# Experts summed by tokens, factors brought to the places by products, one more weight region, wider router products

## The chip, the cores and the metric

The kernel runs on one core of a Trainium2 chip. The metric is the device time of one execution in microseconds (us), as the median of several runs. The engines are TensorE (PE in the rows; its weight loads are PEld), VectorE (DVE), ScalarE (ACT), GpSimd (POOL) and SyncE (SP), which issues all transfers here.

## The reference, cut to what matters

Two transformer-like blocks are applied to a stream of 256 tokens with 1024 features: a gated mixer and a feed-forward part under conditioning, then pooling and sparse attention, cross attention to a memory, and a layer of experts. The change touches mostly the last:

```python
h = rmsnorm(x, ffn_norm)
g_sel = argmax(h @ wg_router + bg)                     # one of 4 groups
e_in  = (h @ we_router + be)[g_sel]                    # 8 experts of that group
top_w = softmax(top2(e_in)) * softmax(g_logits)[g_sel] # two experts a token, with weights
hid   = silu(h @ w_gate[e]) * (h @ w_up[e])            # 1024 -> 256, for each of 32 experts
x     = x + sum over the token's two experts of top_w * (hid @ w_down[e])
```

All is float32. The weights of all 32 experts are read, whichever tokens choose them.

## The kernel before

Weights are read once, in order, from one long array ("stream" in DRAM, the list PLAN) into regions: R0 to R25, 26 buffers of 128 x 2048 float32 (1 MB each, NREG at L247). The same regions hold activations: the stream of tokens by features (xt), its transposed copy (ht), the gathered places (xg) and so on. A region is free again when its last reader is done. Small work buffers are two tiles U (512 wide), tiles s, and T pieces of a region; B are the eight PSUM banks.

All instructions of the program are first recorded and then put in order by a planner (plan, L589, and flush, L763): for each engine it picks the next instruction by modelled times and priorities. PATH (L830) lists seeds that perturb the priorities from pass to pass; the last pass counts. Transfers keep their recorded order on SyncE. A transfer may be issued ahead as long as a region is left for all buffers that come before its use. Where the planner sees a wait on TensorE it puts in fillers, products of a matrix of ones that nobody reads (filler, L795; their rows have L800). As all is issued from one helper, nearly all other rows have L823.

The work around the change: the sum of squares is turned into a norm factor per token by norm_col (L1115), with products of one column. After the cross attention, rf is that factor; the router's products (40 columns: 4 groups, 4 empty, 32 experts) of xt are scaled by it. xt is transposed to ht (L1823), scaled by rf on the way out of PSUM. VectorE chooses the experts (asum marks them), products with a triangle of ones count the places, and places (L1886) makes a 0/1 table s8 of tokens by places: each of 32 experts has CAP = 32 places. There are eight groups of four experts. For each group, experts (L1940) does:

- gather (L1921): products of ht with s8 bring the tokens to their places (xg), features by places;
- the gate and up weights, eight regions, as tiled products (four experts side by side, 32 columns of the array each), silu and product to hid;
- two transposes, then the down weights, four regions, as tiled products to ye, places by features;
- combine (L1934): products of ye with the table of weights (w8 = s8 times the weight of the token, transposed) add into four PSUM banks, features by tokens.

After the last group the sum is added to xt in four parts and written. SyncE reads the number of rounds (more than one only if an expert has over 32 tokens, which does not happen here) at L2029.

Early in the program, the conditioning sums (ada_pe, ada_v) go through a U tile each; group means and head factors are products with constant matrices (blk, sel, dup, perm) from the constants cst.

Of the kernel before, what the change touches and what calls it, by code (L numbers as in the profile page):

```python
# [15 lines left out]
KT = D // 128  # L16
# [7 lines left out]
    ("c", 8), ("norm1_g", 8), ("b_u", 4), ("b_val", 4), ("b_gate", 4), ("taps", TAPS), ("taps4", 96),  # L24
# [7 lines left out]
for _n, _w in VEC:  # L32
# [5 lines left out]
    ("ident", 128), ("e4", 4), ("same", 32), ("blk", 128), ("perm", 128), ("dup", 128), ("triu", 128),  # L38
    ("iota", 32), ("half", 2), ("sel", 512), ("thr", 8),
# [9 lines left out]
def constants():  # L49
# [9 lines left out]
    put("blk", (p[:, None] // 64 == p[None, :] // 64) / 64.0)  # L59
    put("perm", (p[:, None] == (p[None, :] ^ 32)))  # L60
    put("dup", (p[:, None] == p[None, :] % 64))
# [3 lines left out]
    sel = (np.arange(8)[:, None, None] == 2 * np.arange(4)[None, :, None] + p[None, None, :] // 64)  # L65
    put("sel", sel.reshape(8, 512))
# [18 lines left out]
def rope_tables():  # L85
    f = np.float32
    inv = (f(10000.0) ** (-(np.arange(0, 64, 2, dtype=f)) / f(64))).astype(f)
# [4 lines left out]
    return np.concatenate([np.tile(cos, (2, 1)), np.tile(sin, (2, 1))], axis=1).astype(f)  # L92


def layout(v):
# [14 lines left out]
    def rowk(w):  # L110
# [12 lines left out]
        "taps": taps[0], "taps4": taps4,  # L123
# [23 lines left out]
    for name, arg in PLAN:  # L147
# [60 lines left out]
        "wr": wr.reshape(KT, 128, 40).transpose(1, 0, 2), "br": br,  # L208
# [38 lines left out]
NREG = 26  # L247
# [120 lines left out]
def cost(eng, name, args, kw):  # L368
# [7 lines left out]
    if eng == "tensor":  # L376
# [4 lines left out]
        if "tile_position" in kw:  # L381
            return mv.free() * passes / 2.4e3 + 0.01
# [447 lines left out]
PATH = (0, 0, 11, 0, 63, 67, 74, 0, 89, 239)  # L830
# [9 lines left out]
def _build(tc, a, out, ctx):  # L840
# [11 lines left out]
    rec = Recorder(nc, {"R": [region(i) for i in range(NREG)], "U": tiles(2, "U", 512),  # L852
# [71 lines left out]
    inv_d = fixed(1, "inv_d")  # L924
    G.memset(inv_d, 1.0 / D)
    inv_a = fixed(1, "inv_a")
    G.memset(inv_a, 1.0 / DA)
# [151 lines left out]
    class Sums:  # L1079


        def __init__(self):
            self.acc, self.n = [], 0

        def add(self, src):
            i = self.n % 2
            self.n += 1
            if self.n <= 2:
                self.acc.append(buf("T", T))
            acc = self.acc[i]  # L1090
            if self.n <= 2:
                S.activation(out=acc, in_=src, func=AF.Square)
                return
# [4 lines left out]
    def rstd(out_, in_):  # L1098
        S.activation(out=out_, in_=in_, func=AF.Sqrt, bias=eps[0:in_.shape[0], 0:1])
# [15 lines left out]
    def norm_col(accs, inv, r=None):  # L1115
# [7 lines left out]
        rstd(r, ps[:, 0:2])  # L1123
# [124 lines left out]
    def stacked(i):  # L1248


        o = VOFF["taps4"] + 32 * i
        w = view(rtaps[i // 2], 1024 * (i % 2), 32, 32)
        V.tensor_tensor(out=w, in0=cs("same").unsqueeze(1).to_broadcast([128, 32, 32]),
                        in1=cv[:, o:o + 32].unsqueeze(2).to_broadcast([128, 32, 32]), op=ALU.mult)
# [3 lines left out]
    def memory():  # L1258
# [6 lines left out]
        rmem = norm_col(sums.acc, inv_d, rmem_)  # L1265
# [35 lines left out]
    S.activation(out=rb, in_=norm_bc(norm_col(sums.acc, inv_d)), func=AF.Copy)  # L1301
    xr = view(Reg(), 0, KT, T)
    rtaps = [Reg(), Reg()]
    wtaps = [stacked(i) for i in range(3)]
# [43 lines left out]
    def conv_v():  # L1348
        for i in range(TAPS):
            w, src = col("taps", i), ypad[:, i:i + T]  # L1350
# [67 lines left out]
    def mix():  # L1418
# [15 lines left out]
        bc = norm_bc(norm_col(suma.acc, inv_a))  # L1434
# [7 lines left out]
    def gn():  # L1442
        sq4 = view(r1, 0, 4, T)
        for j in range(4):
            ps = bank()[:, 0:T]
            PE.matmul(out=ps, lhsT=cs("blk"), rhs=yc[:, j], start=True, stop=True)
# [10 lines left out]
        normed(y, 4, yc, 4, "on_b", norm_bc(norm_col(sumb.acc, inv_a)))  # L1457
# [26 lines left out]
    r2_ = norm_col(sq2.acc, inv_d)  # L1484
# [39 lines left out]
    rbf = norm_bc(norm_col(sqf.acc, inv_d))  # L1524
# [18 lines left out]
    cosin = view(ri_, 1152, 2, T)  # L1543
    SY.dma_start(out=cosin, in_=a["cosin"].rearrange("p (a n) -> p a n", a=2))
# [4 lines left out]
    rmx = norm_col(sqx.acc, inv_d)  # L1549
# [12 lines left out]
    def rope(dst, src, t=None):  # L1562

        if t is None:
            sw = bank()[:, 0:T]
            PE.matmul(out=sw, lhsT=cs("perm"), rhs=src, start=True, stop=True)
# [9 lines left out]
    def key_index():  # L1576
# [3 lines left out]
        PE.matmul(out=pd, lhsT=cs("dup"), rhs=zk, start=True, stop=True)  # L1580
# [169 lines left out]
    wr, br = view(rq_, 1024, KT, 40), view(rq_, 1024 + KT * 40, 40)  # L1750
    SY.dma_start(out=wr, in_=a["wr"])
    SY.dma_start(out=br, in_=a["br"])
    for k in range(KT):
        V.tensor_scalar(out=wr[:, k], in0=wr[:, k], scalar1=col("fn", k), scalar2=None,
                        op0=ALU.mult)
# [11 lines left out]
    rx_ = norm_col(sq4_.acc, inv_d)  # L1767
# [56 lines left out]
    rf = norm_col(sq5.acc, inv_d)  # L1824
    pl = bank()
    lgt = small3(40, "lgt")
    for t in range(2):
        for k in range(KT):
            PE.matmul(out=pl[:, 64 * t:64 * t + 40], lhsT=xt[:, k, 128 * t:128 * t + 128],
                      rhs=wr[:, k], start=(k == 0), stop=(k == KT - 1))  # L1830
    for t in range(2):
        V.scalar_tensor_tensor(out=lgt[:, t], in0=pl[:, 64 * t:64 * t + 40],
                               scalar=rf[:, t:t + 1], in1=br, op0=ALU.mult, op1=ALU.add)
    for t in range(2):
        for i in range(2):
# [217 lines left out]
```

## Time and profile before

| | us |
|---|---|
| median of 3 runs (736.33 to 739.46) | 736.53 |
| the profiled execution | 738.67 |
| its span, first to last instruction | 737.0 |
| TensorE busy in the span | 703.4 |
| VectorE, ScalarE busy | 415.0, 314.0 |
| moved by the transfers | 212.45 MB |

The span is what the views show; the 1.67 us beside it lie before and after. Busy times overlap, so they are no sum. A matmul's row begins where it is issued, and its end is modelled. The granted clock (PEclk) is the share of the 2.4 GHz that TensorE was given: 1.00 or 0.50.

### The profile page before, as it was taken

The page shows a single profiled execution, that of the slowest core. Times are in us where ns is not written, and L with a number is a line of the kernel's source. Part 1 is how long each engine was busy: PE and PEld are TensorE (multiplying, and loading weights), DVE is VectorE, ACT ScalarE, POOL GpSimd, SP SyncE. Part 2 cuts the span into 40 slices and gives each one's busy share as a digit, 9 for nine tenths or more (in the row PEclk, how much of TensorE's full clock was granted, in tenths as well). Part 3 has the DMA queues.
Part 4 walks back from the last instruction along what each step waited for, and adds up shares of the span by engine and source line. Part 5 has one row for each costly group of instructions (what it writes and reads, how often), then busy time and mean ns, then how long its engine had stood idle before and what let it go on. Part 6 is the DMA issues. An engine that isn't in the chain of part 4 may idle for free.

```text
span 737.0 us, 13178 instructions
## 1 busy us (share of the span) xinstructions
PE 703.4 (95%) x5374; PEld 560.9 (76%) x5374; DVE 415.0 (56%) x873; ACT 314.0 (43%) x595; POOL 3.0 (0%) x18
## 2 busy tenths in 40 slices
PE   9999999999999999999999999999999999978864
PEld 9789677999999999999899868998954454522212
DVE  6769957886677775556786998466622121110001
ACT  6647667544544344445754538366512111110000
POOL 0000000000000000000000000000000000000000
PEclk9999999999999999999999999999899999987787
DMA  8997399599468876444811315973789999999993
GB/s 333 418 419 287 123 403 419 197 416 418 180 223 281 300 292 234 166 163 141 335 68 59 114 58 185 373 296 113 292 324 418 418 419 419 419 419 421 420 415 134
DMA packets 31603, 212.45 MB, mean 288 GB/s; under 512 B 3633, under 2 KB 4017, under 8 KB 7089
## 3 DMA queue, kind: packets, MB, share of 16 engines
q1 hardware_dynamic: 31536, 211.55, 73.7%
q8 instruction: 44, 0.72, 0.4%
q14 instruction: 23, 0.18, 0.1%
HBM read 210.48 MB, written 1.05 MB: 287 GB/s over the span
## 4 chain that ended last, share of the span: by engine, by line
PE 69%; DMA 25%; DVE 2%; ACT 2%; issue 1%; SPq 1%; ACTq 0%
PE B L823 69%; DMA R<-stream 25%; ACT R L823 2%; DVE R L823 1%; SPq L823 1%; DVE s L823 0%; PE B L800 0%; ACT s L823 0%; DVE U L823 0%; DVE pos L823 0%; ACTq L823 0%
## 5 line engine op out<-in xcount | busy, mean ns | idle before, releaser
L823 PE MATMUL B<-R,R 128*128 128x256 f32 (+4 forms) x4376 | 580.1, 374 | 16.8 <-DMA R<-stream 13.1
L823 PEld LDWEIGHTS B<-R,R 128*128 128x128 f32 (+2 forms) x4376 | 434.3, 170 | 99.8 <-issue 42.4
L823 ACT ACTIVATE R<-R 128x1024 fp32r<-128x1024 f32 (+4 forms) x268 | 188.8, 738 | 158.0 <-PE B L823 122.8
L823 DVE TENSOR_TENSOR R<-R,R 128x1024 fp32r<-128x1024 f32 (+3 forms) x214 | 192.9, 928 | 71.5 <-ACT R L823 62.1
L823 DVE TENSOR_TENSOR R<-B,R 128x256 f32<-128x256 f32 (+2 forms) x77 | 32.3, 439 | 77.8 <-ACT R L823 55.1
L823 ACT ACTIVATE R<-B 128x256 f32<-128x256 f32 (+3 forms) x81 | 27.0, 370 | 83.4 <-PE B L823 83.3
L823 ACT ACTIVATE R<-B,cv 128x128 f32<-128x128 f32 (+2 forms) x64 | 26.4, 422 | 69.4 <-PE B L823 68.3
L823 PEld LDWEIGHTS B<-U,R 128*128 128x128 f32 x256 | 32.9, 191 | 22.1 <-issue 15.6
L823 DVE COPY R<-B 128x256 f32<-128x256 f32 (+2 forms) x31 | 14.4, 464 | 60.8 <-PE B L823 60.4
L823 PE MATMUL B<-R 128*128 128x256 f32 (+4 forms) x184 | 46.6, 387 | 1.5 <-ACT R L823 1.5
L823 PEld LDWEIGHTS B<-R 128*128 128x128 f32 (+1 forms) x184 | 29.4, 197 | 22.5 <-issue 13.4
L823 ACT COPY R<-B 128x256 f32<-128x256 f32 (+2 forms) x31 | 12.3, 407 | 69.5 <-PE B L823 69.4
L823 DVE TENSOR_SCALAR R<-B,cv 128x128 f32<-128x128 f32 x32 | 11.2, 350 | 50.3 <-PE B L823 49.8
L823 PE MATMUL B<-U,R 128*128 128x128 f32 x256 | 38.4, 285 | 0.9 <-ACT R L823 0.5
L823 DVE SCALAR_TENSOR_TENSOR U<-R,ca,U 128x512 f32<-128x512 f32 x42 | 31.4, 749 | 1.0
L823 PE MATMUL B<-cst,R 128*128 128x128 f32 (+2 forms) x128 | 22.3, 272 | 4.1 <-DVE R L823 3.0
L823 DVE SCALAR_TENSOR_TENSOR R<-R,cv,R 128x256 f32<-128x256 f32 (+1 forms) x54 | 24.9, 480 | 2.0 <-ACT R L823 1.5
L823 ACT ACT_TABLE_LOAD x19 | 24.4, 1283 | 2.9 <-PE B L823 1.8
L823 PEld LDWEIGHTS B<-cst,R 128*128 128x128 f32 x128 | 18.6, 176 | 7.9 <-DVE R L823 4.5
L823 DVE TENSOR_TENSOR R<-R 128x256 f32<-128x256 f32 x47 | 17.9, 419 | 2.9 <-ACT R L823 2.7
L800 PE MATMUL B<-ones 128*128 128x128 f32 x112 | 17.5, 321 | 1.4 <-POOL inv_h L823 1.4
L800 PEld LDWEIGHTS B<-ones 128*128 128x128 f32 x112 | 16.9, 236 | 1.4 <-POOL inv_h L823 1.4
(123 smaller groups left out, 275.4 us busy)
## 6 DMA issues: line engine op xcount, KB each, us to landing
R<-stream SPq DMA_DIRECT2D x190, 1024.0 KB, 12.4
R<-stream SPq DMA_DIRECT2D x14, 512.0 KB, 13.2
R<-mt SPq DMA_DIRECT2D x2, 512.0 KB, 6.9
R<-xt SPq DMA_DIRECT2D x1, 1024.0 KB, 10.6
out_dram<-R SPq DMA_DIRECT2D x4, 256.0 KB, 3.0
cst<-cst SPq DMA_DIRECT2D x1, 533.0 KB, 18.7
R<-bands SPq DMA_DIRECT2D x1, 320.0 KB, 2.8
R<-cosin SPq DMA_DIRECT2D x1, 256.0 KB, 4.2
```

The lines of the kernel that those rows point to most:

```text
L800: self.nc.tensor.matmul(out=self.pools["B"][k][:, 0:128], lhsT=ones, rhs=ones, start=True, stop=True)
L823: getattr(getattr(self.nc, op.eng), name)(*[real(v) for v in args], **{k: real(v) for k, v in kw.items()})
```

## The change

Regions are 27; the second U tile, the constant matrices blk, perm, dup and sel, the taps in the vector array and the router's small tiles are given up. Norm products have 128 columns of ones instead of one column (the division moves into the square root's scale), and the router's products have 128 columns, of which 40 are used. ht is no longer scaled. In its place, per group, tiled products of s8 with two columns (the token's weight for the expert, and rf) give for every place its weight and factor (by); hid and ye are scaled by these. combine exchanges its operands: the sum is by tokens, 4 x 2 products of 256 columns, and it is added to ht, into a new region taken at the end, so that xt is free after the transposes. s8 is built for each group, in the U tile or a spare part of a region. PATH has other seeds.

```diff
-NREG = 26
+NREG = 27
-PATH = (0, 0, 11, 0, 63, 67, 74, 0, 89, 239)
+PATH = (0, 3, 278, 328, 397, 420)
-    rec = Recorder(nc, {"R": [region(i) for i in range(NREG)], "U": tiles(2, "U", 512),
+    rec = Recorder(nc, {"R": [region(i) for i in range(NREG)], "U": tiles(1, "U", 512),
...
-    def rstd(out_, in_):
-        S.activation(out=out_, in_=in_, func=AF.Sqrt, bias=eps[0:in_.shape[0], 0:1])
+    def rstd(out_, in_, scale=1.0):
+        S.activation(out=out_, in_=in_, func=AF.Sqrt, bias=eps[0:in_.shape[0], 0:1], scale=scale)
...
-                PE.matmul(out=ps[:, t:t + 1], lhsT=acc[:, 128 * t:128 * t + 128], rhs=inv,
-                          start=(i == 0), stop=(i == len(accs) - 1))
+                PE.matmul(out=ps[:, 128 * t:128 * t + 128], lhsT=acc[:, 128 * t:128 * t + 128],
+                          rhs=ones, start=(i == 0), stop=(i == len(accs) - 1))
...
-        PE.matmul(out=ps, lhsT=cs("sel", 128 * j, 128 * j + 128, rows=8), rhs=rt, start=True,
-                  stop=True)
+        with rec.join():
+            for e in range(2):
+                one = cs("ident", 2 * j + e, 2 * j + e + 1, rows=8).to_broadcast([8, 64])
+                PE.matmul(out=ps[64 * e:64 * e + 64], lhsT=one, rhs=rt, start=True, stop=True,
+                          skip_group_check=True)
...
+    taps = view(rtaps[1], 1024, 96 + TAPS)
+    SY.dma_start(out=taps, in_=a["taps"])
...
-            PE.matmul(out=pl[:, 64 * t:64 * t + 40], lhsT=xt[:, k, 128 * t:128 * t + 128],
-                      rhs=wr[:, k], start=(k == 0), stop=(k == KT - 1))
+            PE.matmul(out=pl[:, 128 * t:128 * t + 128], lhsT=xt[:, k, 128 * t:128 * t + 128],
+                      rhs=wr[:, 40 * k:40 * k + 128], start=(k == 0), stop=(k == KT - 1))
...
-            S.activation(out=ht[:, t, 512 * i:512 * i + 512], in_=ps, func=AF.Copy,
-                         scale=rf[:, t:t + 1])
+            S.activation(out=ht[:, t, 512 * i:512 * i + 512], in_=ps, func=AF.Copy)
...
-    def gather(xg, s8, q):
+    def gather(xg, s8, g):
...
+        b = bank()
+        for t in range(2):
+            with rec.join():
+                for e in range(4):
+                    PE.matmul(out=b[32 * e:32 * e + 32, 0:2], lhsT=s8[:, t, e],
+                              rhs=wt[:, t, 4 * g + e:33:32 - 4 * g - e], start=(t == 0),
+                              stop=(t == 1), tile_position=(0, 32 * e), skip_group_check=True)
+        V.tensor_copy(out=by, in_=b[:, 0:2])
...
-        for j in ns:
-            PE.matmul(out=ac[j], lhsT=ye[:, 128 * j:128 * j + 128], rhs=sw,
-                      start=(g == 0 and j % 2 == 0), stop=(g == GROUPS - 1),
-                      skip_group_check=True)
+        for c in ns:
+            for t in range(2):
+                PE.matmul(out=ac.b[c][:, t], lhsT=sw[:, 128 * t:128 * t + 128],
+                          rhs=ye[:, T * c:T * c + T], start=(g == 0 and t == 0),
+                          stop=(g == GROUPS - 1), skip_group_check=True)
...
-            if g % 2 == 0:
-                for t in range(2):
-                    V.tensor_tensor(out=w8[:, t], in0=s8q[:, t],
-                                    in1=wt[:, t, 4 * g:4 * g + 8].unsqueeze(2).to_broadcast(
-                                        [128, 8, CAP]), op=ALU.mult)
...
-            S.activation(out=hid, in_=pg[:, 0:256], func=AF.Silu)
-            V.tensor_tensor(out=hid, in0=pg[:, 256:512], in1=hid, op=ALU.mult)
+            S.activation(out=hid, in_=pg[:, 0:256], func=AF.Silu, scale=by[:, 1:2])
+            V.scalar_tensor_tensor(out=hid, in0=pg[:, 256:512], scalar=by[:, 1:2], in1=hid,
+                                   op0=ALU.mult, op1=ALU.mult)
...
-                S.copy(out=ye[:, 0:512], in_=pd[0])
-                V.tensor_copy(out=ye[:, 512:1024], in_=pd[1])
+                S.activation(out=ye[:, 0:512], in_=pd[0], func=AF.Copy, scale=by[:, 0:1])
+                V.tensor_scalar(out=ye[:, 512:1024], in0=pd[1], scalar1=by[:, 0:1], scalar2=None,
+                                op0=ALU.mult)
...
-                V.tensor_tensor(out=xt[:, 2 * c:2 * c + 2], in0=ac.b[c], in1=xt[:, 2 * c:2 * c + 2],
-                                op=ALU.add)
-                SY.dma_start(out=out[:, 2 * c:2 * c + 2], in_=xt[:, 2 * c:2 * c + 2])
+                V.tensor_tensor(out=done[:, c], in0=ac.b[c],
+                                in1=res[:, c] if res else ht[:, :, T * c:T * c + T], op=ALU.add)
+                SY.dma_start(out=out[:, c], in_=done[:, c])
```

The group means (blk) and the copy of the index key to both halves (dup) become pairs of half-width products in the same way as the head factors above.

## Rows read from the trace of the kernel before

**Rows 1.** The page: busy time of each engine, and tenths in 40 slices.

```profile
PE 703.4 (95%) x5374; PEld 560.9 (76%) x5374; DVE 415.0 (56%) x873; ACT 314.0 (43%) x595; POOL 3.0 (0%) x18
...
PE   9999999999999999999999999999999999978864
...
DMA  8997399599468876444811315973789999999993
```

**Rows 2.** The chain that ended last: start us, us, what.

```profile
363.33 118.59 PE B L823 x862
...
554.50 18.90 DMA R<-stream
...
710.67 14.16 DMA R<-stream
...
724.88 3.49 PE B L823 x16
```

**Rows 3.** SyncE's timeline from 536.5 us: start, us, engine, instruction, count.

```profile
536.87 174.13 SPq L823 DMA_DIRECT2D R<-stream  x77
```

**Rows 4.** Windows: stretch, us, busy us of each engine, PEclk, DMA share, GB/s.

```profile
350.90:354.30 3.40, 3.40 (x10) 2.66 (x9) 2.30 (x6) 1.17 (x2) 0.00 (x0) 0.50 1.03 431
521.60:525.00 3.40, 3.40 (x33) 3.40 (x32) 2.87 (x9) 2.69 (x5) 0.00 (x0) 1.00 0.80 243
525.00:531.80 6.80, 6.80 (x34) 6.80 (x34) 3.66 (x27) 3.51 (x6) 0.00 (x0) 0.50 0.92 387
531.80:534.00 2.20, 1.80 (x17) 1.70 (x16) 0.77 (x3) 1.55 (x6) 0.00 (x0) 0.99 0.04 15
534.00:554.00 20.00, 19.98 (x172) 10.31 (x176) 4.92 (x22) 4.00 (x9) 0.00 (x0) 1.00 0.81 325
554.00:653.00 99.00, 98.25 (x730) 50.22 (x720) 20.22 (x51) 15.34 (x40) 0.00 (x0) 1.00 1.01 419
653.00:725.00 72.00, 53.88 (x308) 15.57 (x312) 5.73 (x11) 4.07 (x10) 0.00 (x0) 0.79 0.99 406
725.00:737.00 12.00, 3.35 (x16) 1.92 (x13) 1.81 (x3) 0.00 (x0) 0.00 (x0) 0.56 0.15 50
```

**Rows 5.** TensorE's timeline, 500 to 534.5 us: start, us, instructions, tile, count.

```profile
501.47 1.28 PE L800 MATMUL B<-ones 128*128 128x128 f32 x10
...
521.29 3.31 PE L823 MATMUL B<-R,R 128*128 128x40 f32 x28
...
524.88 1.32 PE L823 MATMUL B<-inv_d,R 128*128 128x1 f32 x6
...
526.91 3.65 PE L823 MATMUL B<-cst,R 128*128 128x128 f32 x16
530.36 2.20 PE L800 MATMUL B<-ones 128*128 128x128 f32 x12
532.40 0.31 PE L823 MATMUL B<-asum,cst 128*128 128x32 f32 x2
```

**Rows 6.** VectorE's timeline, 526 to 535 us, cut to two instructions.

```profile
530.47 0.22 DVE L823 TENSOR_TENSOR asum<-am,a 128x64 f32<-128x64 f32 x1
...
533.45 0.76 DVE L823 TENSOR_TENSOR U<-slot,pos 128x256 f32<-128x256 f32 x2
```

**Rows 7.** Groups by form from 534 us: busy us, mean ns, idle before.

```profile
L823 PE MATMUL B<-R,R 128*32 128x512 f32 x736 | 101.5, 656 | 11.0 <-DMA R<-stream 9.9 <-issue 0.6 <-DVE R L823 0.5
...
L823 PE MATMUL B<-R,R 128*32 128x256 f32 x64 | 4.5, 386 | 3.4 <-DMA R<-stream 2.9 <-DVE R L823 0.5
```

**Rows 8.** Tile U: duration ns, first and last start us, forms.

```profile
L823 PE MATMUL B<-ones,U x48: 164/250/250, 201.9 to 347.4; 128*128 128x1 f32 x48
...
L823 SPq DMA_DIRECT2D U<-pw x1: 383/383/383, 324.3 to 324.3; - x1
```

**Rows 9.** What SyncE waited for: us in total, times, longest.

```profile
SPq L2029 <- DVE wt L823: 12.1, 1, 12.1
```

**Rows 10.** TensorE's weight loads from 537.5 us: start, us, count, idle before.

```profile
538.46 1.19 PEld L823 LDWEIGHTS B<-U,R 128*128 128x128 f32 x10 [0.84 <-issue]
```

More of the change, by code (lines that the diff above doesn't have):

```diff
@@ L37 @@
 CST = [
-    ("ident", 128), ("e4", 4), ("same", 32), ("blk", 128), ("perm", 128), ("dup", 128), ("triu", 128),
-    ("iota", 32), ("half", 2), ("sel", 512), ("thr", 8),
+    ("ident", 128), ("e4", 4), ("same", 32), ("triu", 128), ("iota", 32), ("half", 2), ("thr", 8),
 ]
@@ L207, in layout @@
         "cosin": rope_tables(), "bands": bands(), "stream": stream,
-        "wr": wr.reshape(KT, 128, 40).transpose(1, 0, 2), "br": br,
+        "taps": np.concatenate([taps4, taps[0]], axis=1),
+        "wr": np.concatenate([wr.reshape(KT, 128, 40).transpose(1, 0, 2).reshape(128, -1),
+                              np.zeros((128, 88), np.float32), br], axis=1),
         "pw": g["pool_w_2"][0].transpose(1, 0, 2),
@@ L1264, in memory @@
             sums.add(mt[:, k])
-        rmem = norm_col(sums.acc, inv_d, rmem_)
+        rmem = norm_col(sums.acc, D, rmem_)
         rmem2 = square(rmem)
@@ L1445, in gn @@
             ps = bank()[:, 0:T]
-            PE.matmul(out=ps, lhsT=cs("blk"), rhs=yc[:, j], start=True, stop=True)
+            with rec.join():
+                for e in range(2):
+                    PE.matmul(out=ps[64 * e:64 * e + 64],
+                              lhsT=cs("half", e, e + 1).to_broadcast([128, 64]),
+                              rhs=yc[:, j], start=True, stop=True, skip_group_check=True)
             V.tensor_tensor(out=yc[:, j], in0=yc[:, j], in1=ps, op=ALU.subtract)
@@ L1565, in rope @@
             sw = bank()[:, 0:T]
-            PE.matmul(out=sw, lhsT=cs("perm"), rhs=src, start=True, stop=True)
+            PE.matmul(out=sw, lhsT=perm, rhs=src, start=True, stop=True)
             t = ta()
@@ L1579, in key_index @@
         pd = bank()[:, 0:T]
-        PE.matmul(out=pd, lhsT=cs("dup"), rhs=zk, start=True, stop=True)
+        with rec.join():
+            for e in range(2):
+                PE.matmul(out=pd[64 * e:64 * e + 64], lhsT=cs("ident", 0, 64), rhs=zk, start=True,
+                          stop=True, skip_group_check=True)
         S.activation(out=kd, in_=pd, func=AF.Copy, scale=col("ik_norm"))
@@ L1839, in _build @@
                              in_=xt[:, 4 * i + kk, 128 * t:128 * t + 128], identity=ident)
-            S.activation(out=ht[:, t, 512 * i:512 * i + 512], in_=ps, func=AF.Copy,
-                         scale=rf[:, t:t + 1])
-    am, wt, pos, a2 = (small3(32, n) for n in ("am", "wt", "pos", "a2"))
-    asum, far = small3(32, "asum"), small3(32, "far")
-    m8, i8, e8, j8 = (small3(8, "m8"), small3(8, "i8", U32), small3(8, "e8"),
-                      small3(8, "j8", U32))
-    gi, ng, ex, g4, ei, pw_ = (small3(4, "gi"), small3(4, "ng"), small3(4, "ex"),
-                               small3(4, "g4"), small3(8, "ei"), small3(2, "pw_"))
-    eg = Recorder.shaped(fixed(64, "eg", F32, False), (2, 4, 8))
+            S.activation(out=ht[:, t, 512 * i:512 * i + 512], in_=ps, func=AF.Copy)
+    am, a2, asum, far = (temp(32) for i in range(4))
+    pos = small3(32, "pos")
+    m8, e8, i8, j8 = temp(8), temp(8), temp(8, U32), temp(8, U32)
+    gi, ng, ex, g4, ei, pw_ = (temp(n) for n in (4, 4, 4, 4, 8, 2))
+    eg = view(rq_, used[0], 2, 4, 8)
     def over(v, n):
@@ L2010, in quarter @@
                     product(ps, view(regs[c], 1024 * f, 4, T), f)
-                (V.tensor_copy if c % 2 else S.copy)(out=ye[:, T * c:T * c + T], in_=ps)
+                to = ye[:, T * c:T * c + T]
+                if c % 2:
+                    V.tensor_scalar(out=to, in0=ps, scalar1=by[:, 0:1], scalar2=None, op0=ALU.mult)
+                else:
+                    S.activation(out=to, in_=ps, func=AF.Copy, scale=by[:, 0:1])
+            done = res or view(Reg(), 0, 4, 2, T)
             rec.series = {}
@@ L2051 @@
     y = r.results[0]["out_0_dram"]
[L2052 removed]
+    return np.ascontiguousarray(y.transpose(2, 0, 1, 3)).reshape(1, T, D)
```

132 lines of the change are left out of this document (65 added, 67 removed).

## The prediction

> **What bounds the kernel now.** I read the page's 40 slices first [rows 1]. TensorE is busy nine tenths or more of nearly every slice, and the DMA queue is full in the last ten, so the slices alone don't say which of the two sets the end. The chain of waits does [rows 2]: up to 554.5 us it runs almost wholly over TensorE, from there over waits for weight transfers, one behind another, until the last of them lands at 724.84 (710.67 + 14.16); TensorE's last run and the way out take the 12.2 us to the end of the span. The kernel thus has a front bound by TensorE and an expert stage bound by transfers.
>
> SyncE's timeline shows when the refilling of the expert stage starts [rows 3]: 77 transfers are issued from 536.87 on. The last four regions are loaded in halves, so these are 73 regions. The experts need 96 (8 groups of 12), so 23 were issued earlier. That fits the count of regions: 26, less the stream, its transposed copy and the gathered places, which are all alive at the first gather. The windows tell the rest [rows 4]. Between 531.8 and 534.0 the queue is idle (share 0.04): all that fits is loaded. From 554 on it moves 419 GB/s, that is 2.50 us for a region of 1.049 MB, and it never pauses. TensorE is full until 653 (98.25 of 99 us) because it eats the 23 regions of lead; then it waits (53.88 of 72 us). So the end is the start of the refilling, plus 2.50 us for each region that isn't there yet, plus a fixed tail. Two things move it: how many regions are loaded ahead, and when the first gather lets go of a region. TensorE's work inside the stage is covered up to a margin, worked out below.
>
> **Two more regions ahead.** There are 27 regions (places of the constants, of a second U tile and of the small router tiles are given up for it). The final sum is now taken onto the transposed copy, so the stream's region is free after the transposes; the router's small tiles lie in the region of the router weights, which is dead before the gather. At the first gather two regions are taken instead of three: 25 for weights, 2 more than 23. Both can load in the idle gap before the refilling. That leaves 71 regions behind it: 2 x 2.50 = 5.0 us less. Bounds: 2.5, if the second comes so late that the refilling queues behind it, and 5.0. I take 5.0, since the stream's last readers, the transposes, end about 3 us before the first gather.
>
> **The router stretch.** From 521.6 to 525.0 TensorE is busy the whole 3.40 us at the full clock of 2.4 GHz, and yet from 525.0 to 531.8 it was granted 0.50, that is 1.2 GHz [rows 4]. What it did before the fall is in its timeline: router products 40 wide, and products of one column for the norm [rows 5]. In the long stretch 554 to 653, with products 128 to 512 wide, the grant stays at 1.00. The change makes both kinds 128 wide. The width itself costs nothing: 28 instructions 40 wide took 3.31 us, 0.118 each, ten fillers 128 wide 1.28 us, 0.128 each with the last one's tail (a product is two instructions). The Trainium skill speaks against it: "TensorE: Matmul & The Clock Gate", section "Back-to-back issue gap", gives a product of 1 to 64 columns some 60 cycles and one of 128 columns 134. By that, an estimate, 40 instructions would take 74 cycles or 31 ns more each, and the sum would be 1.2 us higher; the trace shows no such step, and the sum goes by it.
>
> At half clock a transpose took 3.65 / 16 = 0.228 us, twice the 0.118 to 0.128 of the full one. If the clock stays up, the nine norm and router instructions between 525.0 and 526.9 save 0.1 each, and the choice table (asum), ready at 530.69, is ready at 529.8 [rows 6]. Now TensorE reaches the counting products only at 532.40, as 16 transposes and 12 fillers at half clock stand ahead [rows 5]; they would be through at 529 to 530, and the counting starts right behind the table, at 530.0: 2.4 us earlier. The first place table is built for one group, not two: its 0.76 us fall to between 0.38 and 0.76; I take 0.2 off. Together 2.6 us. Bounds: nothing, if the clock falls all the same, and 3.4 (6.8 us at half clock). What is late next is the first gather's own 2 us, as before.
>
> **Work added inside the expert stage.** Each group gets 16 tiled instructions of two columns (8 products) that carry weight and norm factor to the places. Nearest rows: tiled instructions cost 101.5 / 736 = 0.138 us at 512 columns and 4.5 / 64 = 0.070 at 256 [rows 7]. Two columns lie between nothing and 0.128 each; I take 0.070: 1.1 us a group, 9 in all. The cover: TensorE's busy time from 534 to 725 is 19.98 + 98.25 + 53.88 = 172.1 us [rows 4]. With the first gather 2.6 earlier it would end at 531.4 + 172.1 = 703.5 without any wait, and the last transfer comes at 724.84 - 7.6 = 717.2: 13.7 us of cover, 1.7 a group. Costed at nothing, then; above 1.7 a group all of it shows. The sum by tokens has the same 8 products of 256 columns a group with the operands exchanged, and the DVE products of weights with places fall away while scales ride on evictions that exist: nothing, since VectorE is busy 20.2 of 99 us there. ScalarE's copies of the transposes no longer wait for the norm; they were not last at the gather.
>
> **The front.** Products that used constant matrices (group means, head factors, the copy to both halves) become pairs of half-width ones: 13 products more. At nothing if halves run side by side, at most 13 x 2 x 0.128 = 3.3 us; I take 0. The norm products become 128 wide at the price of rows 5. Three more stretches of 3.4 us at half clock stand in the front, one of them at 350.9 to 354.3 [rows 4]; each is worth at most 1.7 us. They follow norm products too, but also products of 1 to 4 columns that stay: I take 1.0 for the three, bounds 0 and 5.1. The constants' transfer shrinks and the taps get one of their own: nothing, TensorE's chain covers transfers there; uncovered, one issue, 0.4 us. With one U tile the conditioning sums take turns, and the transfer of the pool weights, issued at 324.3, has to wait for the last conditioning products at 347.4 [rows 8]; one weight region and the bands queue behind it on SyncE, all for use after the attention: nothing. SyncE's read of the round count, where it sat 12.1 us [rows 9], comes after the last early transfer, as before; if the 25th region queues behind it, that is the 2.5 bound above. The order of instructions is searched anew with other seeds: TensorE was idle only 534 - (703.4 - 172.1 - 3.35) = 6.1 us in the front, so little is to be gained; I take 0, plus or minus 3.
>
> **Sum.** The profiled execution took 738.67 us (span 737.0 and 1.67 around it). 738.67 - 5.0 - 2.6 - 1.0 = 730.1. It lay 2.14 above the median of 736.53, so the median after is 728.0.
>
> **Rivals.** (A) The clock falls at the router all the same. For it: the wide products are few, and narrow ones remain close by. Then 738.67 - 5.0 - 0.2 - 2.14 = 731.3. (B) Wide norm products hold the clock at all four places: 5.0 + 2.6 + 5.1 off, 723.8. Against it: TensorE has waits at some of them, where it gains nothing. (C) Slower: TensorE becomes the bound in the expert stage. If the two-column instructions cost as much as wide ones, 16 x 0.128 = 2.0, and stand between full-width products, the weight loads pause 0.84 us at a change from tiles to the full array [rows 10]; two such changes make 3.7 a group, 30 us in all. TensorE would end at 703.5 + 30 = 733.5, 8.7 after today's last transfer: 736.53 + 8.7 = 745.2. It sets the end from 1.7 a group on and is slower than today from (724.84 - 703.5) / 8 = 2.7. Beside it stands the Trainium skill, "TensorEngine Tiling (Array Packing)", section "Key Properties": a change of tiling mode drains the engine; the pause of 0.84 agrees. Against it: these products have the shape of the weight products and can stand beside them, and a narrow tile is cheap by rows 7. (D) The new order loses 3 to 8 us in the front: 731 to 736. For it: the front is bound by TensorE, where each lost us counts; against it: the work there is the same.
>
> **Chances.** Forecast 0.50 (725.5 to 730.5), A 0.18, B 0.15, C 0.06, D 0.11. Runs of the kernel before spread over 0.4%, so some 0.5%, 3.7 us, is what can be told from no change: faster is below 732.8, slower above 740.2. The forecast, B, three quarters of A and some of D are faster: 0.81; C is slower: 0.06; the rest, 0.13, is the same. The range leaves out C, the far ends of B and D: 722.5 to 734.0.
>
> **What would show it.** Right: 71 whole regions issued from the first gather on, starting near 534; a grant of 1.00 from 521 to 532 in the front's last stretch; TensorE's waits in the stage starting later than 653 (it has more lead); the last landing near 717. Wrong: 23 or 24 regions ahead; half clock at the router; TensorE full to the end, with no wait for transfers after 653 (C); a first gather later than 534 (D).

## The result, and the profile after

The changed kernel takes 729.46 us (median of 4, 727.65 to 730.66) against 737.19 for the kernel before beside it: ratio 0.9888, 95% interval 0.9856 to 0.9921. Forecast was 728.0, range 722.5 to 734.0. The profiled execution took 730.66, its span 728.9 against 737.0: 8.1 us less. The predicted sum was 8.6, but the way there was not quite the predicted one. In all that follows, rows of the changed kernel carry L821 (fillers L798).

The page of the changed kernel, busy time of the engines and the granted clock in 40 slices, beside [rows 1]:

```profile
PE 695.4 (95%) x5524; PEld 554.6 (76%) x5524; DVE 415.9 (57%) x881; ACT 313.6 (43%) x594; POOL 2.5 (0%) x16
...
PEclk9999999999999999999999999999999999998788
```

The end of its chain of waits, as [rows 2]. Weights still set the end, from 646 us on instead of 554:

```profile
620.29 25.82 PE B L821 x194
646.11 19.82 DMA R<-stream
...
704.89 12.53 DMA R<-stream
717.42 0.04 issue
717.46 2.58 PE B L821 x16
```

SyncE's timeline from 530 us, as [rows 3]. 75 transfers, the last eight of them halves, make 71 regions, as predicted; 73 before.

```profile
535.12 170.10 SPq L821 DMA_DIRECT2D R<-stream  x75
```

Windows of the changed kernel, columns as in [rows 4]. The grant is 1.00 at 350.9 and from 521 to 530, where it had been 0.50, and half in a new place, 530.3 to 533.8. TensorE is busy to 653 and beyond; its first wait for weights in this stage ends at 665.98.

```profile
350.90:354.30 3.40, 3.40 (x24) 3.07 (x23) 0.77 (x4) 1.98 (x3) 0.00 (x0) 1.00 0.00 0
521.00:525.00 4.00, 4.00 (x39) 4.00 (x38) 2.23 (x14) 2.04 (x4) 0.00 (x0) 1.00 0.88 348
525.00:530.00 5.00, 3.75 (x33) 3.45 (x31) 3.82 (x26) 3.60 (x10) 0.00 (x0) 1.00 1.02 421
530.30:533.80 3.50, 3.50 (x20) 2.43 (x22) 1.24 (x7) 0.37 (x1) 0.00 (x0) 0.51 0.34 143
554.00:653.00 99.00, 98.90 (x808) 50.93 (x808) 20.46 (x59) 17.24 (x40) 0.00 (x0) 1.00 1.01 420
653.00:717.50 64.50, 48.29 (x318) 15.22 (x318) 5.69 (x11) 4.75 (x10) 0.00 (x0) 0.84 0.98 403
```

TensorE's timeline at the router, as [rows 5]: the transposes, the last counting products, the first gather, the first expert products.

```profile
523.75 1.91 PE L821 MATMUL B<-cst,R 128*128 128x128 f32 x16
...
528.37 0.61 PE L821 MATMUL B<-R,ones 128*128 128x32 f32 x4
530.03 2.60 PE L821 MATMUL B<-U,R 128*128 128x128 f32 x12 [1.05 <-DVE U L821]
532.56 3.99 PE L821 MATMUL B<-R,R 128*32 128x512 f32 x28
```

The 16 transposes take 1.91 us (3.65 before), but then TensorE stands still for 1.05 us ahead of the gather, and the gather's 12 instructions take 2.60 us where 14 had taken 1.80. VectorE's timeline, beside [rows 6], shows what the gather waits for:

```profile
527.65 0.19 DVE L821 TENSOR_SCALAR R<-R 128x64 f32<-128x64 f32 x1
528.65 0.17 DVE L821 TENSOR_SCALAR R<-R 128x2 f32<-128x2 f32 x1 [0.80 <-ACT R L821]
...
529.33 0.21 DVE L821 TENSOR_TENSOR pos<-R,B 128x64 f32<-128x64 f32 x1
529.46 0.21 DVE L821 TENSOR_TENSOR R<-R 128x64 f32<-128x64 f32 x1
529.60 0.48 DVE L821 TENSOR_TENSOR U<-slot,pos 128x128 f32<-128x128 f32 x2
```

The counts (pos) stand behind four small instructions for the weights, the first of which waits 0.80 us for ScalarE; the new order put them there.

With these rows the 8.1 us can be laid out along the path. Before, the last addition to the stream ended at 524.47, the first gather began at 534.02, refilling at 536.87.

| stretch | before | after | difference | predicted |
|---|---|---|---|---|
| start to the last addition (520.38 + 1.76 after) | 524.47 | 522.14 | -2.33 | -1.0 |
| last addition to first gather | 9.55 | 7.89 | -1.66 | -2.6 |
| first gather to first refill | 2.85 | 5.09 | +2.24 | 0 |
| first refill to last landing | 187.97 | 182.30 | -5.67 | -5.0 |
| last landing to the end (clock 0.56 before, 0.82 after) | 12.16 | 11.48 | -0.68 | 0 |

The last landing is 717.42; the prediction says 717.2, without the 1.0 of the front that its sum counts, 716.2 with it. The sum is right because errors of its terms cancelled; the experiments look behind them. They are numbered in the order in which they ran and told by subject. Each was timed against the kernel before on the same chip; experiments 1 to 4, 5 to 8 and 9 to 12 shared one, and across these groups ratios are compared. That is rough: the changed kernel itself gave 0.9888 and, in experiment 9, 0.9914, 2 us apart. Where a few us matter, the profiles carry the argument.

### The profile page after: what moved, and what is told of

The parts are those of the page before. It is cut to its first block, busy times and chain, and to the rows that moved or that the text cites. A ratio compares the mean times of both kernels' runs of the same rounds, so it can differ in the third digit from the quotient of the medians.

```text
span 728.9 us, 13510 instructions
## 1 busy us (share of the span) xinstructions
PE 695.4 (95%) x5524; PEld 554.6 (76%) x5524; DVE 415.9 (57%) x881; ACT 313.6 (43%) x594; POOL 2.5 (0%) x16
## 3 DMA queue, kind: packets, MB, share of 16 engines
HBM read 210.14 MB, written 1.05 MB: 290 GB/s over the span
## 4 chain that ended last, share of the span: by engine, by line
PE 82%; DMA 12%; DVE 3%; ACT 1%; issue 1%; SPq 0%; DVEq 0%; ACTq 0%
PE B L821 82%; DMA R<-stream 12%; DVE R L821 2%; ACT R L821 1%; DVE s L821 0%; DVE U L821 0%; ACT L821 0%; SPq L821 0%; ACT U L821 0%; ACT wt L821 0%; ACT s L821 0%; DVE g L821 0%; DVE wt L821 0%; DVE cond L821 0%; DVE pos L821 0%
## 5 line engine op out<-in xcount | busy, mean ns | idle before, releaser
L821 PE MATMUL B<-R,R 128*128 128x256 f32 (+5 forms) x4528 | 596.5, 368 | 16.7 <-DMA R<-stream 13.7
L821 PEld LDWEIGHTS B<-R,R 128*128 128x128 f32 (+2 forms) x4528 | 452.9, 170 | 107.2 <-issue 49.3
L821 ACT ACTIVATE R<-R 128x1024 fp32r<-128x1024 f32 (+5 forms) x271 | 188.4, 732 | 154.4 <-PE B L821 107.5
L821 DVE TENSOR_TENSOR R<-R,R 128x1024 fp32r<-128x1024 f32 (+3 forms) x214 | 192.0, 928 | 71.3 <-ACT R L821 69.5
L821 ACT ACTIVATE R<-B,cv 128x128 f32<-128x128 f32 (+2 forms) x64 | 26.1, 421 | 69.2 <-PE B L821 68.2
L821 DVE TENSOR_SCALAR R<-B,cv 128x128 f32<-128x128 f32 x32 | 11.2, 350 | 63.5 <-PE B L821 61.5
L821 PE MATMUL B<-R 128*128 128x256 f32 (+4 forms) x186 | 44.4, 369 | 0.9 <-ACT R L821 0.9
L821 ACT ACTIVATE R<-B,s 128x512 f32<-128x512 f32 (+1 forms) x21 | 12.2, 586 | 76.4 <-PE B L821 75.1
L821 ACT ACTIVATE R<-B 128x256 f32<-128x256 f32 (+4 forms) x77 | 26.5, 380 | 41.9 <-PE B L821 39.0
L821 DVE TENSOR_TENSOR R<-B,R 128x256 f32<-128x256 f32 (+2 forms) x69 | 28.8, 441 | 26.1 <-PE B L821 16.3
L821 PEld LDWEIGHTS B<-R 128*128 128x128 f32 (+1 forms) x186 | 28.3, 189 | 14.6 <-issue 9.1
L821 DVE SCALAR_TENSOR_TENSOR R<-B,s,R 128x256 f32<-128x256 f32 (+1 forms) x24 | 9.5, 433 | 46.9 <-ACT R L821 46.1
L821 DVE SCALAR_TENSOR_TENSOR U<-R,ca,U 128x512 f32<-128x512 f32 x42 | 31.4, 747 | 0.5
L821 PEld LDWEIGHTS B<-U,R 128*128 128x128 f32 x128 | 17.6, 200 | 15.1 <-issue 9.5
L821 PE MATMUL B<-cst,R 128*128 128x128 f32 (+1 forms) x136 | 22.7, 262 | 4.1 <-DVE R L821 3.8
L821 PEld LDWEIGHTS B<-cst,R 128*128 128x128 f32 x136 | 17.6, 162 | 11.0 <-DVE R L821 5.0
L821 PE MATMUL B<-U,R 128*128 128x128 f32 x128 | 21.5, 300 | 1.0 <-DVE U L821 1.0
L821 DVE TENSOR_TENSOR R<-R 128x256 f32<-128x256 f32 (+2 forms) x54 | 19.3, 389 | 3.2 <-ACT R L821 2.7
L821 ACT COPY R<-B 128x256 f32<-128x256 f32 (+1 forms) x22 | 7.7, 354 | 30.3 <-PE B L821 30.1
L821 DVE TENSOR_SCALAR R<-B,s 128x512 f32<-128x512 f32 (+1 forms) x9 | 6.2, 691 | 21.9 <-PE B L821 21.9
L798 PE MATMUL B<-ones 128*128 128x128 f32 x108 | 14.6, 296 | 1.3 <-POOL inv_h L821 1.3
## 6 DMA issues: line engine op xcount, KB each, us to landing
R<-stream SPq DMA_DIRECT2D x14, 512.0 KB, 12.6
```

Source lines behind the costliest of these rows:

```text
L798: self.nc.tensor.matmul(out=self.pools["B"][k][:, 0:128], lhsT=ones, rhs=ones, start=True, stop=True)
L821: getattr(getattr(self.nc, op.eng), name)(*[real(v) for v in args], **{k: real(v) for k, v in kw.items()})
```

## The experiments

**1. Two regions later.** The 24th and 25th weight region go behind the 26th in SyncE's order.

```diff
+        weights = sy[-104:-4]
+        for x in weights[23:25]:
+            order.remove(x)
+        i = order.index(weights[25]) + 1
+        order[i:i] = weights[23:25]
         for x in order:
```

> The changed kernel with one edit: the 24th and 25th expert weight region are loaded behind the 26th, so that only 23 regions are there before the first gather, as in the kernel before; everything else, order and instructions, is as changed. If the time after 554 us is the start of the refilling plus 2.50 us for each region behind it (the step of the prediction), the last landing moves from 717.4 to about 722.4 and the time rises by about 5.0 us over the changed kernel: ratio to the kernel before near 0.9955. The rival, that the gain came from clock and order alone and the two transfers are hidden anyway, expects no rise: ratio 0.989.

Measured: 733.61, ratio 0.9928 (0.9903 to 0.9953), 0.4% or 3 us above the changed kernel. The last landing came at 720.01, 2.59 later. That is less than 5.0 for a reason which the profile shows: refilling began at 532.76, 2.36 earlier than in the changed kernel, as the clock fell neither at 35 us nor in the gather. 717.42 - 2.36 + 2 x 2.50 = 720.06.

```profile
530.78 3.42 PE L828 MATMUL B<-R,R 128*32 128x512 f32 x28
```
```profile
532.76 175.02 SPq L828 DMA_DIRECT2D R<-stream  x77
```

**8. Four regions later.** The same with `weights[21:25]` behind `weights[27]`.

> The changed kernel with the 22nd to 25th weight region loaded behind the 28th transfer: 21 regions ahead of the first gather instead of 25. By 2.50 us a region behind the start of the refilling the last landing comes 10.0 us later than in the changed kernel, less up to 2.4 us if the clock stays up in the first gather, as it did with 23: 725.0 to 727.4, time 7.6 to 10.0 us more, ratio 0.998 to 1.002. The rival, that regions are worth less than the transfer's 2.50 us each (the first experiment measured 1.5 to 2.1 for each of two), expects 6 to 8 us: ratio 0.996 to 0.999, with the same last landing as the clock's part explains, or none.

Measured: 740.6, ratio 1.0024 (1.0009 to 1.0039): 1.36% or 10.0 us above the changed kernel's 0.9888. Refilling began at 534.13, 0.99 earlier, and the last landing is at 726.43: 717.42 - 0.99 + 4 x 2.50 = 726.43. A region ahead is worth its 2.50 us, to 0.05 us in both experiments. The rival, a smaller worth, falls; in the profiled execution the small rise of experiment 1 was the clock's.

**2. Narrow products in the new order.** The changed kernel, same order and transfers, with the norm products one column and the router products 40 columns wide. (The lines show what is issued, here and in experiment 3; the planner still goes by the widths of the unedited kernel, so its order stays.)

```diff
-    PE.matmul(out=ps[:, 128 * t:128 * t + 128], ..., rhs=ones, ...)
+    PE.matmul(out=ps[:, 128 * t:128 * t + 1], ..., rhs=ones[:, 0:1], ...)
...
-    PE.matmul(out=pl[:, 128 * t:128 * t + 128], ..., rhs=wr[:, 40 * k:40 * k + 128], ...)
+    PE.matmul(out=pl[:, 128 * t:128 * t + 40], ..., rhs=wr[:, 40 * k:40 * k + 40], ...)
```

> The changed kernel with the norm products one column wide and the router products 40 wide, as before the change, in the same order on every engine and with the same transfers. If the width keeps the clock up at the router, the grant falls to 0.50 again between about 525 and 532, the first gather comes about 2 us later, some of the 2.3 us that the front gained are lost too, and the time rises by 1.5 to 3.5 us over the changed kernel: ratio 0.991 to 0.994. The rival, that the new order and not the width keeps the clock, expects no change: ratio 0.989.

Measured: 731.09, ratio 0.9883 (0.9857 to 0.9908): no change, as the rival said, though not for its reason. Windows of this kernel:

```profile
114.00:160.00 46.00, 45.09 (x347) 38.53 (x342) 35.02 (x75) 25.43 (x49) 0.00 (x0) 0.93 0.90 347
525.00:530.00 5.00, 5.00 (x36) 5.00 (x35) 3.28 (x26) 3.80 (x9) 0.00 (x0) 0.73 1.04 411
530.00:534.00 4.00, 2.88 (x28) 2.38 (x31) 2.72 (x16) 0.89 (x3) 0.00 (x0) 1.00 0.64 238
```

The clock does fall at the router again (0.50 from 524.2 to 527.7), but then not in the first gather, which runs at 1.00. It falls at 121.5 and 152.2 too. In none of the nine profiles with the wide products in this order did it fall at these three places, which speaks for the width there; but the changed kernel's execution has its own two half-clock stretches, at 35 us and in the gather, and refilling starts at 535.42 here, 535.12 there. The half clock comes in other places, and no gain in time shows.

**3. Wide products in the old order.** The kernel before, same order and 26 regions, with both kinds 128 wide (the division moved into the square root's scale, zeros behind the router's weights).

```diff
-                PE.matmul(out=ps[:, t:t + 1], ..., rhs=inv, ...)
+                PE.matmul(out=ps[:, 128 * t:128 * t + 128], ..., rhs=ones, ...)
...
-                      rhs=wr[:, k], start=(k == 0), stop=(k == KT - 1))
+                      rhs=wide[:, 40 * k:40 * k + 128], start=(k == 0), stop=(k == KT - 1))
```

> The kernel before with norm products and router products 128 wide and nothing else changed: same order, same 26 regions, 23 of them loaded ahead. If width keeps the clock up, the grant is 1.00 from 525.0 to 531.8 and perhaps at 350.9 too, the first gather starts 2 to 4 us earlier and the time falls by 2 to 4 us: ratio 0.9945 to 0.997. The rival, that width alone does nothing, expects 1.000.

Measured: 735.07, ratio 0.996 (0.994 to 0.9981): 2.9 us faster. Window and first refill of this kernel:

```profile
524.50:531.50 7.00, 5.92 (x52) 5.65 (x51) 5.18 (x36) 4.73 (x11) 0.00 (x0) 1.00 0.83 350
```
```profile
533.63 174.46 SPq L826 DMA_DIRECT2D R<-stream  x77
```

The grant is 1.00 where [rows 4] had 0.50, with the same instructions in the same order and transfers beside them. Of five half-clock stretches of 3.4 us ahead of the refilling (two of them joined at the router) one is left, at 117. The last addition ends at 523.53 (-0.94), the gather begins 7.24 later (9.55 before, -2.31), refilling 2.86 after that: 3.24 us in all. So the prediction's two clock terms, 1.0 and 2.4, fit this kernel, while in the changed one they came with two counterweights. The first is one execution's, though: experiment 11, which has the same instructions up to the router, had its last addition at 525.53, 2.0 later.

**11 and 12. Which of the two.** Experiment 3 with the norm products alone, and with the router products alone, 128 wide.

> The kernel before with the norm products alone 128 wide; the router products stay 40 wide. If the norm products are what keeps the clock, the grant is up at the router as in the third experiment and in two of the three half-clock stretches further ahead, and the time falls by the same 3 us: ratio 0.996. If both are needed, the clock falls at the router still (3.4 or 6.8 us at half) and 1 to 2 us remain: ratio 0.998. If the router's width alone does it: 1.000.

> The kernel before with the router products alone 128 wide; the norm products stay one column wide. If the router products are what keeps the clock at the router, the grant is 1.00 from 525 on while the three stretches further ahead stay at half clock: first gather 2 to 2.5 us earlier, ratio 0.997. If the norm products do it, nothing changes: ratio 1.000.

Measured: norm alone 734.65, ratio 0.9969 (0.9948 to 0.9991); router alone 737.56, ratio 1.001 (0.9991 to 1.0029). Windows of the first, then of the second:

```profile
504.00:510.00 6.00, 5.71 (x27) 4.97 (x28) 3.19 (x10) 2.60 (x9) 0.00 (x0) 0.72 0.00 0
524.50:531.50 7.00, 6.29 (x57) 6.10 (x57) 4.69 (x31) 5.12 (x8) 0.00 (x0) 1.00 0.97 384
```
```profile
110.00:125.00 15.00, 15.00 (x94) 8.81 (x91) 9.86 (x22) 12.04 (x23) 0.00 (x0) 0.77 1.01 419
148.00:160.00 12.00, 11.08 (x73) 9.97 (x66) 8.12 (x24) 5.32 (x12) 0.00 (x0) 0.72 1.01 392
350.00:358.00 8.00, 7.30 (x35) 5.81 (x33) 6.81 (x16) 5.44 (x8) 0.00 (x0) 0.79 1.01 376
524.50:531.50 7.00, 7.00 (x65) 7.00 (x65) 5.16 (x24) 4.58 (x11) 0.00 (x0) 1.00 0.91 338
```

Either kind alone kept the clock up at the router in its profile, and from the last addition to the first gather it took 7.24 and 7.12 us (9.55 before). With the norm products alone a new place fell, at 505.3. With narrow norm products the three places further ahead fell to half clock, at 114.8 and 152.3 for twice as long as before; the last addition came 3.5 us later than before, and nothing was gained. In time only the norm products, which stand in four places, show a gain; the router's, in one, are worth nothing that these runs can tell. Whether the longer stretches belong to that kernel or to that execution is open.

**4 and 7. More work for TensorE in the expert stage.** Behind the two-column products of each group 7 (then 20) products of ones, 128 wide, which nobody reads.

```diff
+        rec.ops[-1].calls += [("matmul", (), dict(out=b[:, 128:256], lhsT=ones, rhs=ones, ...))] * EXTRA
         V.tensor_copy(out=by, in_=b[:, 0:2])
```

> The changed kernel with seven more products of a matrix of ones, 128 wide, behind the two-column products of each of the eight groups; nobody reads them. Seven products are 14 instructions of about 0.11 us: about 1.55 us a group, 12 us in all. If transfers set the end and the cover of TensorE's work in the expert stage is over 12 us, the time stays as it is: ratio 0.989, with TensorE's steady waits for weights starting about 12 us later. If TensorE sets the end of the stage (rival C), all 12 us show: ratio 1.005.

> The changed kernel with 20 extra products of ones in each of the eight groups (in the earlier experiment 7): 40 instructions of about 0.11 us, 4.4 us a group, 35 us in all. By the prediction's cover of 13.7 us TensorE would set the end and 35 - 13.7 = about 21 us would show: ratio 1.017. If the cover is larger by the time that TensorE spends at half clock between 660 and 725 (some 27 us of the stage, of which half comes back when it has no more waits), 13 us would be hidden more: about 8 us show, ratio 0.999. Rival: transfers set the end still, nothing shows: 0.988.

Measured: 7 products 730.16, ratio 0.9872 (0.9845 to 0.9900), nothing shows; 20 products 742.43, ratio 1.004 (1.0026 to 1.0054). One window of the changed kernel and the same of that with 7, then the groups from 530 us and the chain's end of that with 20:

```profile
660.00:725.00 65.00, 43.82 (x276) 13.52 (x268) 6.46 (x12) 3.33 (x7) 0.00 (x0) 0.84 0.90 368
```
```profile
660.00:725.00 65.00, 49.40 (x395) 22.07 (x393) 8.57 (x18) 5.49 (x12) 0.00 (x0) 0.99 0.90 368
```
```profile
L822 PE MATMUL B<-R,R 128*32 128x512 f32 x736 | 88.8, 599 | 0.6 <-issue 0.6
L822 PE MATMUL B<-ones 128*128 128x128 f32 x320 | 37.9, 278 | 0.0
```
```profile
725.61 8.00 PE B L822 x80
```

With 20 no weight is waited for, and TensorE sets the end. It got 37.9 us more work and its span rose by 13.4 (742.3 - 728.9), so 24.5 us were covered, not 13.7. The difference is nearly all clock: in the changed kernel TensorE ran part of this stage at half clock (0.84 from 660 to 725), with 20 products it didn't (1.00). With seven it still waited for weights (busy 49.40 of the 65 us) and had 0.99 all the same, so waits alone don't bring the clock down. The same 736 tiled products took 99.4 us in the changed kernel and take 88.8 here, 10.6 less, of 10.8 to be explained. Rival C's point of decision was therefore not 1.7 but 3.1 us a group.

**5. Place counts first.** The changed kernel with pos and the first place table ahead of the five small weight instructions. VectorE's order:

```diff
-    ng3 + 1, ng3 * ng1, 1 / ng3, pw1, pos, am * pw0, U, U, a2 * pw1
+    pos, U, U, ng3 + 1, ng3 * ng1, 1 / ng3, pw1, am * pw0, a2 * pw1
```

> The changed kernel with VectorE's order altered at the router: the place counts (pos) and the first place table (U) stand ahead of five small instructions for the weights, four of which waited 0.8 us for ScalarE's exponential. If pos is late only because it queues behind them, pos starts about 0.6 to 0.7 us earlier (it has its products by 528.6), the first gather too, TensorE's pause of 1.05 us ahead of it shrinks to about 0.4, and the time falls by 0.6 us; if that pause is also why the clock falls in the first gather (at 530.35), the fall goes away and another 1.7 us is gained: last landing 715 to 717. The rival, that the first gather waits for something else, expects no change: last landing 717.4.

**6. Products in the pause.** The changed kernel with four more products of ones on TensorE just ahead of the first gather (x is its first product).

```diff
+            order.insert(order.index(x), (4, place[x[0].calls[0][2]["out"].buf]))
```

> The changed kernel with four more products of ones that nobody reads (8 instructions, about 0.9 us) put on TensorE into its pause of 1.05 us ahead of the first gather. If the clock falls in the first gather because TensorE paused just before, the grant stays at 1.00 there, the 12 gather instructions take about 1.6 us instead of 2.6, the refilling starts 1.7 to 2.2 us earlier and the time falls as much: last landing near 715.5. The rival, that the fall has nothing to do with the pause (the transfers beside it, or what came before), expects the fall to stay and no gain: last landing 717.4 to 717.6.

Measured: 728.76, ratio 0.9852 (0.983 to 0.9873), and 729.32, ratio 0.9862 (0.9839 to 0.9886). In both the first gather ran at full clock, 12 instructions in 1.58 us, and refilling started at 532.10 and 532.37 instead of 535.12; the last landings are 714.43 and 714.83. In time neither stands clear of the changed kernel's 0.9888 (0.9856 to 0.9921).

**10 and 9. Both, beside the changed kernel.** Experiment 5 with one more product of ones in the 0.28 us that were left, and the changed kernel again.

> The changed kernel with the place counts and the first place table ahead of the small weight instructions on VectorE (as in the fifth experiment) and one more product of ones (2 instructions, 0.23 us) in the pause of 0.28 us that was left ahead of the first gather. If the pauses ahead of the gather cost the clock there, it stays up as in the fifth and sixth experiments and the kernel is about 2.5 us faster than the changed one: ratio 0.3% below that of the changed kernel beside it, last landing 714 to 715.5. The rival, that those two profiles were only lucky, expects half clock in the gather and 0.1% or less.

> The changed kernel once more, unaltered, to stand beside the next ones on the same chip: ratio 0.986 to 0.990. If the halving of the clock in the first gather is a property of this order and not of one execution, it is there again (it was in three of three profiles with a pause of 1.05 us and transfers beside it), 12 gather instructions taking 2.4 to 2.9 us.

Measured: 728.65 (727.46 to 729.87), ratio 0.9898 (0.9875 to 0.9921), and 730.27 (728.78 to 730.78), ratio 0.9914 (0.9891 to 0.9936): 1.6 us. The ratios' intervals overlap; of the six runs of the changed kernel five lie above all six of the other. It beats both kernels, by little. TensorE's timelines, this kernel, then the changed one again:

```profile
522.28 1.91 PE L840 MATMUL B<-cst,R 128*128 128x128 f32 x16
...
527.80 1.58 PE L840 MATMUL B<-U,R 128*128 128x128 f32 x12
529.71 3.42 PE L840 MATMUL B<-R,R 128*32 128x512 f32 x28 [0.33 <-DVE nr L840]
```
```profile
523.78 1.91 PE L821 MATMUL B<-cst,R 128*128 128x128 f32 x16
...
530.06 2.81 PE L821 MATMUL B<-U,R 128*128 128x128 f32 x12 [1.05 <-DVE U L821]
532.80 3.78 PE L821 MATMUL B<-R,R 128*32 128x512 f32 x28
```

Refilling starts at 531.69, 3.46 before 535.15. Of that 1.50 were there at the transposes already, where the kernels are the same (a half-clock stretch at 35 us, in the one execution and not in the other). From there on the edited kernel was shorter by 0.76 up to the gather (5.52 from the transposes instead of 6.28) and by 1.20 from there to the refilling (3.89 instead of 5.09): 1.96, and 1.6 measured. The half clock in the gather was there again in the second profile of the changed kernel, so it is no matter of a single execution; whether the edits took it away is asked next.

What makes it fall there is open. Of the nine profiles with the wide products in this order it fell in the four with the pause of 1.05 us and transfers running beside it (the changed kernel twice, 7 and 20 products); not in the two with the pause and no transfers (two and four regions later, DMA share 0.01 and 0.02 from 526 to 530), nor in the three with transfers and the pause closed. But experiment 2 had a pause of 1.12 us and transfers beside it (share 0.87 from 530 to 532), and its gather ran at full clock, behind a half-clock stretch 4 us earlier. And the four that fell had also fallen at 35 us, while the three with the pause closed had not. The changed kernel, then experiment 5:

```profile
35.00:39.00 4.00, 4.00 (x23) 3.42 (x25) 4.00 (x22) 3.39 (x9) 0.00 (x0) 0.57 1.00 418
```
```profile
35.00:39.00 4.00, 4.00 (x37) 2.85 (x37) 4.00 (x20) 3.84 (x10) 0.00 (x0) 1.00 1.02 420
```

So no profile has the pause closed behind a fall at 35 us, and it is not shown that closing the pause kept the clock up. What the new order of VectorE gains by itself is the shorter way to the gather, 0.76.

## Why the prediction was right, and where its terms were off

**Two regions.** Right in mechanism and size: 71 regions behind, 2.50 us each, shown by experiments 1 and 8. The lower bound of 2.5 did not come about: the 25th region was issued at 525.73, 9.4 us ahead of the refilling. The row in the table is 5.67; experiment 1, with 73 regions as before, needs 187.25 from first refill to last landing, so 4.95 of it are the two regions. The other 0.72 is not explained; with the same 73 regions, profiles of the old order need from 187.42 (experiment 11) to 187.97.

**The router stretch.** The clock stayed up from 521 to 530.3, not to 532 as the sign asked, so rival A falls at the place it named. But the term was mis-sized: 2.6 predicted, 1.66 up to the gather, and then 2.24 given back inside it. The step that failed is "What is late next is the first gather's own 2 us, as before". Late next were VectorE's instructions for the counts, behind a wait for ScalarE that the new order put ahead of them (undone in experiment 5), and the gather ran at half clock. At full clock the stretch from gather to refilling takes 3.49 (experiments 1, 2, 6 and 8), so 1.60 of the 2.24 are clock. The other 0.64 is order: at full clock the first refill is issued 1.98 us after the first expert products, behind 16 of them (530.78 to 532.76 in experiment 1), where it came 1.12 after them, behind eight (535.75 to 536.87). Had the prediction asked what else queues on VectorE between the choice and the counts, a wait there would have been a rival.

**The front.** 2.33 against 1.0, and the bounds of 0 and 5.1 hold; where it comes from is settled only in part. Experiment 3 puts 0.94 on the norm products, but executions alike up to the router differ by 2.0 there (experiments 3 and 11), and the changed kernel's profile bears a half-clock stretch at 35 us that others of its order don't. By-form groups show work that is gone: the 36 instructions with constant matrices (10.2 us) give way to 20 half-width ones (2.8), while the ordinary products of that shape grow from 2888 to 2912 (379.0 to 385.3), some 1.1 less; in the same windows (to 520 us, before to 525) the fillers fell from 15.3 to 12.6 and the 512-wide products grew from 57.5 to 59.0. The pairs for the head factors, 32 instructions, take 4.1 us where 16 took 4.0: the choice of nothing, not 3.3, was right. Rival D's loss did not come; what the order alone is worth was not tried. Rival B falls too: the grant held at all four of its places, but fell at new ones (35 and 530 us).

**The width at no price.** Right. From the first norm product to the first transpose 14 instructions follow one another at full clock. All are 128 wide in experiment 3, the six of the router 40 wide in experiment 11, the eight of the norm one column wide in experiment 12:

```profile
523.59 0.39 PE L826 MATMUL B<-ones,R 128*128 128x128 f32 x2
...
525.15 1.91 PE L826 MATMUL B<-cst,R 128*128 128x128 f32 x16
```
```profile
525.50 0.47 PE L826 MATMUL B<-ones,R 128*128 128x128 f32 x2
...
527.06 1.94 PE L826 MATMUL B<-cst,R 128*128 128x128 f32 x16
```
```profile
528.05 0.28 PE L826 MATMUL B<-inv_d,R 128*128 128x1 f32 x2
...
529.62 1.91 PE L826 MATMUL B<-cst,R 128*128 128x128 f32 x16
```

They take 1.56, 1.56 and 1.57 us, 0.11 each whatever the width. The rule of the Trainium skill that was set aside, "TensorE: Matmul & The Clock Gate", section "Back-to-back issue gap", gives some 60 and 134 cycles, an estimated 31 ns between them; these rows show no such step.

**Work in the expert stage.** At nothing, right: the 128 two-column instructions took 1.4 + 1.3 = 2.7 us, not 9 (0.021 each, not 0.070), no pause stands at the changes of tile shape behind them (16 of them at 652.24, the next full-width product 0.22 later), and the cover was 24.5, not 13.7. The weight loads, which paused 0.84 us in [rows 10], go on there at once:

```profile
652.24 0.19 PEld L821 LDWEIGHTS B<-wt,U 128*32 128x32 f32 x12 [0.30 <-issue]
652.45 0.80 PEld L821 LDWEIGHTS B<-R,R 128*128 128x128 f32 x12
```

Behind the 512-wide tiled products they pause 0.84 us still (at 654.95), so the pause that the prediction took for the price of such a change is not paid at each. Groups of the changed kernel from 530 us:

```profile
L821 PE MATMUL B<-R,R 128*32 128x512 f32 x736 | 99.4, 638 | 11.7 <-DMA R<-stream 11.0 <-issue 0.6 <-ACT R L821 0.2
...
L821 PE MATMUL B<-wt,R 128*32 128x2 f32 x64 | 1.4, 175 | 0.0
L821 PE MATMUL B<-wt,U 128*32 128x2 f32 x64 | 1.3, 172 | 0.0
```

Rival C was wrong in its price as well as in its point of decision.

**The tail.** The fixed 12.2 us shrank by 0.68, as the grant at the end was 0.82 instead of 0.56 and the last 16 products took 2.58 us instead of 3.49 [rows 2]; not foreseen.

## What to carry to other kernels

Where transfers set the end of a stage, count what is loaded when refilling starts: each buffer more is worth its own transfer time, here to a few hundredths of a us, while work added on the covered engine costs nothing up to a margin that a load of idle products measures. A stretch that is made faster hands its wait to the next in-order queue: look there for what has just become late. Judge a clock effect by where the half-clock stretches went, not by whether the one under study is gone, and by more than one execution.

## What the runs showed of the hardware that was not expected

- The same instructions get another clock from one execution to the next: from 35 to 39 us the grant was 0.57 to 0.60 in five profiles with the changed kernel's order and wide products and 1.00 in four, although nothing differed up to there. The transposes began at 523.9 on average in the five and at 522.6 in the four, 1.3 us apart.
- More work made TensorE's other work faster: with seven idle products a group the grant from 660 to 725 us was 0.99 instead of 0.84, and the end did not move (last landing 717.01).
- Two-column tiled instructions on four column groups take 0.021 us each, a sixth of the 0.135 of those 512 wide (99.4 / 736).
